# Four more pairs of projections by seven half products, and the order of their steps, in a one-core encoder layer

## The chip, the cores and the metric

The kernel runs on one core of one Trainium2 chip. The metric is the device time of one execution in microseconds (us). The engines of the core are named as in the profile: PE multiplies matrices (PEld is its weight load, which overlaps), DVE and ACT work element by element, POOL copies small things and issues the transfers that add to their destination, SP issues all other transfers.

## The reference: one encoder layer on 512 tokens

One post-norm layer of width 1024 on 512 tokens, in float32. Two attentions stand side by side, each has its own output projection, two sigmoid gates merge them, then come the output projection, a layer norm, a SwiGLU block of width 2816 and a second layer norm. Cut to what matters:

```python
proj = h @ w_in[l]                                   # 1024 -> 1536 (A) + 3 * 768 (B)
qa, ka, va, qb, kb, vb = jnp.split(proj, SPLITS, axis=-1)
qa, ka, qb, kb = rope_partial(...)                   # first 16 of each head's 64 columns
o_a = windowed_gqa_sink(qa, ka, va, a_sink[l])       # 16 heads, |i-j| <= 128, a sink per head
o_b = dilated_mixture(qb, kb, vb)                    # 4 slots x 3 dilations 1, 4, 16
g_a, g_b = jnp.split(jax.nn.sigmoid(h @ w_gate[l] + b_gate[l]), N_BRANCH, axis=-1)
mixed = g_a * (o_a @ w_br_a[l]) + g_b * (o_b @ w_br_b[l])
h = layer_norm(DN_ALPHA * h + mixed @ w_out[l], ln1_g[l], ln1_b[l])
f = (jax.nn.silu(h @ w_ff_gate[l]) * (h @ w_ff_up[l])) @ w_ff_down[l]
h = layer_norm(DN_ALPHA * h + f, ln2_g[l], ln2_b[l])
```

## The kernel before: a planned stream of matmuls

Every float32 operand of a product is split into a high part of reduced precision and the rest (a copy, mostly on ACT, then a subtraction on DVE), and a product of two of them is three matmuls: high by high, high by low, low by high. So each 128 by 512 piece of weights costs a transfer, a copy and a subtraction before PE can use it.

The weights lie packed in units of 128 output columns (a [128, 1024] block, two halves of 512). The projections of the first part of the layer come in two forms.

- A **plain unit** (`in_sbuf`, `dense_q`, `gate`, through `feat_x` and `feat_k`, L523 to L525) multiplies 8 pieces of 128 weights with all 512 tokens: 8 x 3 = 24 matmuls of 512 columns. Its weights are 4 tiles: two halves, each with a high and a low part.
- A **pair** (`pair_x`, L639 to L641) makes two units at once by Strassen's scheme on 2 x 2 blocks: seven products instead of eight, each of 4 x 3 = 12 matmuls of 256 columns, 84 in all. Before the products stand the sums of weight blocks: S1 and S3 are loaded as one block, to which a second transfer from POOL's queue adds another (`load_sum`, L387), S2 = S1 + A11 and S4 = A12 + S2 are DVE additions (`form`, through `tt`, L544), and seven operands are split (`parts`: ACT L373, DVE L544). Behind the products, four pieces are kept by ACT (`keep`, L647), and DVE joins them with one addition of 512 columns and one of 256 (L544, L662). The sums of token blocks are made once (`x_forms`).

Nothing in the program's order is written by hand line by line. Each operation is given to a list scheduler (`Program.op`) with its engine or engines, a cost, the tiles it reads and writes, and a due time: the PE time of all work noted so far (`pr.T`) plus an offset. Weights have an offset of -130 us, so they may be fetched and split that far ahead. `Program.run` then goes through a reckoned time and gives every free engine the ready operation with the earliest due time whose tiles find room; the resulting order of each engine is the program, and on the chip each engine keeps to it. Room is counted: 85 slots of [128, 512] float32, by classes (staging of weights `ws`, split weights `whl`, attention, the rest), and 8 PSUM banks by classes. Where a tile is counted in, `slab.tile` or `psum.tile` is called with one tag for all 85 slots or all 8 banks, and the pool chooses the place. The reckoned times include the transfers: on SP's queue `o.done = moved + (LATE if 95 < now < 150 else 2.4 ...)`, on POOL's 3.2 us (6.2 us late in the first part) behind the bytes.

The sequence of steps is the string `ORDER`: V, q and k of attention A (`VA`, `q1`, `k1`), its units `A0` to `A3`, pairs `P:`, turning of rows for the rotary part (`R`, `turn_rows`: 16 of each 64 rows of the tiles are gathered by SP, shuffled and multiplied by DVE, and put back by SP), the values of attention B (`V12`, `V0`), its units `B0` to `B3`, gates (`g`), fetching of A's output (`O`). Before the change it names eight pairs. Attention units issue small copies of the sink logits on POOL (L1020) ahead of their first scores, tied to the unit's first score matmul; scores, their reduction on DVE, the exponent on ACT, normalising, transposes on PE (L973, L988), splits and the product with the values follow one another.

Behind the first part come the branch projections (L523 to L525 with other operands), the output projection (L1480 to L1482), and the SwiGLU block, whose products by pairs of units (L1690 to L1692) and chunks (L1901 to L1903) are not touched.

## Time and profile before

| what | value |
|---|---|
| runs | 728.09, 728.14, 729.88 us; median 728.14 us |
| profiled execution, from its first to its last instruction | 725.8 us; the runs' median is 2.3 us longer |
| PE | 717.3 us busy, 99%, 4767 matmuls |
| DVE | 655.6 us busy, 90% |
| ACT | 471.4 us busy, 65% |
| POOL | 134.0 us busy, 18% |
| transfers | 140.30 MB, mean 193 GB/s |
| granted PE clock | 0.996 of full speed |

A matmul's busy time is from its start to a modelled end, and neighbours overlap, so what a matmul costs PE is the distance from its start to the next start, not its duration. DVE's and ACT's instructions overlap by some 0.1 us as well. "Idle" of an engine is a stretch minus its busy time in that stretch.

### The profile page before, as it was taken

To read this page: it belongs to the slowest core of one execution; us is meant where nothing else is said; L and a number is where in the kernel's file an instruction comes from. 1 tells how busy PE (TensorE), PEld (TensorE's weight loads), DVE (VectorE), ACT (ScalarE), POOL (GpSimd) and SP (SyncE) were. 2 spreads that over 40 slices of the span, in tenths; PEclk is the share of its full clock that TensorE was granted. 3 is DMA by queue.
4 is the path that set the end of the run, shared out by engine and by line. 5 is a ranking of instruction groups with operands and counts; after the bars stand their busy time and mean duration, and the time that the engine had idled before them with its cause. 6 is when DMAs were issued, how large, how long until landed. Compare 5 with 4: busy or idle time off the path is not lost.

```text
span 725.8 us, 14412 instructions
## 1 busy us (share of the span) xinstructions
PE 717.3 (99%) x4767; PEld 666.2 (92%) x4767; DVE 655.6 (90%) x1408; ACT 471.4 (65%) x1077; POOL 134.0 (18%) x297
## 2 busy tenths in 40 slices
PE   9999999999999999999999999999999999999995
PEld 7889999989988888988888999999999999999985
DVE  6999999889997898898967898899999999899987
ACT  5757798868778665666534666756666566666821
POOL 0021211111100731450020021111112211212000
PEclk9999999999999999999999999999999999999998
DMA  8978788856577689965681499676888888979302
GB/s 256 309 155 202 191 213 246 211 135 172 170 192 185 160 228 253 309 217 185 216 209 44 116 267 228 154 199 155 200 254 212 193 215 225 258 184 200 97 30 87
DMA packets 88010, 140.30 MB, mean 193 GB/s; under 512 B 11136, under 2 KB 24064, under 8 KB 87936
## 3 DMA queue, kind: packets, MB, share of 16 engines
q1 hardware_dynamic: 74336, 114.87, 51.7%
q0 software_dynamic: 13328, 24.39, 20.5%
q8 instruction: 37, 0.61, 0.3%
q14 instruction: 37, 0.30, 0.1%
q10 hardware_dynamic: 272, 0.13, 0.1%
HBM read 114.97 MB, written 7.60 MB: 169 GB/s over the span
## 4 chain that ended last, share of the span: by engine, by line
PE 99%; DVE 1%; DVEq 0%; issue 0%
PE ps L1692 10%; PE ps L1691 9%; PE ps L1690 9%; PE ps L523 9%; PE ps L524 9%; PE ps L525 9%; PE ps L1901 4%; PE ps L1903 4%; PE ps L1902 4%; PE ps L641 3%; PE ps L640 3%; PE ps L639 3%; PE ps L973 3%; PE ps L1480 3%; PE ps L1481 3%; PE ps L1482 3%
## 5 line engine op out<-in xcount | busy, mean ns | idle before, releaser
L373 ACT ACTIVATE sl<-sl 128x512 fp32r<-128x512 f32 (+3 forms) x419 | 230.8, 583 | 59.7 <-DVE sl L544 31.1
L544 DVE TENSOR_TENSOR sl<-sl,sl 128x512 fp32r<-128x512 f32 (+3 forms) x378 | 222.4, 621 | 5.1 <-ACT sl L373 3.4
L373 ACT ACTIVATE sl<-ps 128x256 f32<-128x256 f32 (+5 forms) x209 | 88.7, 445 | 91.6 <-PE ps L1692 56.8
L387 POOL DMA_DIRECT2D sl<-wpack x60 | 53.1, 885 | 342.9 <-DMA sl<-wpack 118.2
L1691 PE MATMUL ps<-sl,sl 128*128 128x256 f32 x352 | 96.8, 275 | 0.0
L1692 PE MATMUL ps<-sl,sl 128*128 128x256 f32 x352 | 96.8, 275 | 0.0
L1690 PE MATMUL ps<-sl,sl 128*128 128x256 f32 x352 | 96.8, 275 | 0.0
L523 PE MATMUL ps<-x,sl 128*128 128x512 f32 (+1 forms) x241 | 93.9, 389 | 0.0
L525 PE MATMUL ps<-x,sl 128*128 128x512 f32 (+1 forms) x241 | 91.4, 379 | 0.0
L524 PE MATMUL ps<-x,sl 128*128 128x512 f32 (+1 forms) x209 | 79.5, 380 | 0.0
L1690 PE MATMUL ps<-x,sl 128*128 128x256 f32 x264 | 72.6, 275 | 0.0
L1691 PE MATMUL ps<-x,sl 128*128 128x256 f32 x264 | 72.6, 275 | 0.0
L1692 PE MATMUL ps<-x,sl 128*128 128x256 f32 x264 | 72.6, 275 | 0.0
L1691 PEld LDWEIGHTS ps<-sl,sl 128*128 128x128 f32 x352 | 67.6, 192 | 0.1
L1690 PEld LDWEIGHTS ps<-sl,sl 128*128 128x128 f32 x352 | 67.6, 192 | 0.1
L1692 PEld LDWEIGHTS ps<-sl,sl 128*128 128x128 f32 x352 | 67.6, 192 | 0.0
L399 DVE TENSOR_TENSOR sl<-sl,sl 128x512 fp32r<-128x512 f32 x94 | 62.8, 682 | 1.8 <-ACT sl L373 1.3
L525 PEld LDWEIGHTS ps<-x,sl 128*128 128x128 f32 x241 | 45.9, 190 | 6.5
L1690 PEld LDWEIGHTS ps<-x,sl 128*128 128x128 f32 x264 | 50.6, 192 | 0.4
L1691 PEld LDWEIGHTS ps<-x,sl 128*128 128x128 f32 x264 | 50.6, 192 | 0.4
L523 PEld LDWEIGHTS ps<-x,sl 128*128 128x128 f32 x241 | 46.0, 191 | 5.4 <-ACT sl L373 0.3
L1692 PEld LDWEIGHTS ps<-x,sl 128*128 128x128 f32 x264 | 50.7, 192 | 0.0
(172 smaller groups left out, 1851.0 us busy)
## 6 DMA issues: line engine op xcount, KB each, us to landing
sl<-wpack SPq DMA_DIRECT2D x249, 256.0 KB, 3.9
sl<-wpack POOLq DMA_DIRECT2D x60, 256.0 KB, 5.3
sl<-sl SPq DMA_DIRECT2D x110, 128.0 KB, 3.1
wf<-wpack SPq DMA_DIRECT2D x51, 256.0 KB, 5.2
wf<-wpack POOLq DMA_DIRECT2D x24, 256.0 KB, 6.2
oa<-sl SPq DMA_DIRECT2D x32, 128.0 KB, 3.6
sl<-sl SPq DMA_DIRECT2D x68, 32.0 KB, 2.6
sl<-oa SPq DMA_DIRECT2D x8, 256.0 KB, 5.1
```

Source lines behind the costliest of these rows:

```text
L373: nc.scalar.activation(dst, src, AF.Copy)
L387: op([(POOL, 1.0)], lambda e: nc.gpsimd.dma_start(b.t, src2, accum_op=ALU.add), reads=[b], writes=[b], prio=prio, moves=1.65)
L399: op([(DVE, dve(S))], lambda e: nc.vector.tensor_tensor(l.t, src.t, f32(h.t), op=ALU.subtract), reads=[src, h], writes=[l], prio=prio, abs ...
L523: mm(o, a, x0, start=(k == 0 and begins), stop=False, skip_group_check=split)
L524: mm(o, a, x1, start=False, stop=False, skip_group_check=split)
L525: mm(o, b, x0, start=False, stop=(k == nk - 1), skip_group_check=split)
L544: op([(DVE, dve(w))], lambda e: nc.vector.tensor_tensor(dst(), x(), y(), op=o), reads=reads, writes=writes, prio=prio)
L1690: mm(o, wh, pairs(bh[k]()), start=(first and k == 0), stop=False, skip_group_check=True)
L1691: mm(o, wh, pairs(bl[k]()), start=False, stop=False, skip_group_check=True)
L1692: mm(o, wl, pairs(bh[k]()), start=False, stop=(k == 3), skip_group_check=True)
L1901: mm(ps.t, x0, pairs(w[0].t), start=(first and m == 0), stop=False, skip_group_check=True)
L1902: mm(ps.t, x0, pairs(w[1].t), start=False, stop=False, skip_group_check=True)
```

## The change

1. **Twelve pairs instead of eight.** The string `ORDER` is new. The eight units that were plain and are now in pairs are `q3`, `K10`, `Q10`, `Q11`, `Q12` and three gates; the twelve pairs are `q3,g`, `k1,q4`, `q5,Q01`, `q6,q7`, `g,g`, `g,Q00`, `g,K00`, `g,K01`, `Q02,K02`, `K10,Q10`, `Q12,Q11`, `g,g`. Two plain units of 24 matmuls of 512 columns each become one pair of 84 of 256, four times.
2. **Each step may carry an offset** (`@-471`) that is added to the due times of its operations while it is noted.
3. **Three pairs are marked `D:`.** Their sums S2 and S4 are not added by DVE but by a transfer from POOL's queue between two tiles in SBUF (`accum_op`, L624 of the new file), six in all. Two `r` steps gather the shuffled rows by 8-row transfers in place of DVE's shuffle.
4. **Transfers are reckoned longer**: the latency part by 1.3 while the reckoned time is under 380 us (`LONG`), and four transposes as 0.436 us instead of 0.36. These change the order that the scheduler makes, nothing else.
5. **Places are given out by the scheduler**: each of the 85 slots and 8 banks (and of the two small pools) has its own tag, and a tile is made in the place that has been free longest. Limits of some classes change by one or two.

New functions that no step of the new `ORDER` calls (`half_values`, a form of the last sums by transfers) are left out here.

```diff
-SPARE, SPARE2 = 12, 12
+SPARE, SPARE2 = (10, 12)
+LONG = 1.3
 ORDER = """
-VA q1 A0 q2 q3 g X P:k1,q4 R A1 P:q5,g P:q6,q7 R A2 P:g,g A3 P:g,g L P:Q00,K00 R V12 P:Q01,K01 R P:Q02,K02 R V0 B0 Q10 K10 R Q11 K11 R B1 O O Q12 K12 R O O B2 B3 O O O O g8
+q1@-471 X@-159 VA A0@-92 q2@-21 P:q3,g@-28 R@-36 D:k1,q4@-16 R@89 P:q5,Q01@-152 D:q6,q7@-32 r@680 D:g,g P:g,Q00@-10 L P:g,K00@-42 A1@-39
+R@180 V12@-5 P:g,K01@-30 R@22 P:Q02,K02@-15 R@-10 A2@-71 A3@-67 V0@36 P:K10,Q10@-17 B0@-44 O@-1217 O@-237 R@-587 K11@-20 B1@-33 P:Q12,Q11@-22
+R@-393 K12@-28 g@-17 O@-15 g@1 O@-37 g@13 P:g,g@-18 r@-237 O@-28 O@-26 B2@-290 O@62 g@12 g@-12 B3@-224 O@122 g@-26
 """
-FORMS = -60.0
-VAL = -100.0
-OA_AFTER = (0, 0, 0, 0, 0, 0, 0, 0)
+FORMS = -165.0
+VAL = -130.0
+OA_AFTER = (0, 0, 0, 0, 0, 1, 1, 0)
-N_WSA, N_WHLA = 8, 16
+N_WSA, N_WHLA = (8, 18)
...
                         if b.tile is None:
-                            b.tile = b.make()
+                            if b.keys[0] in self.rooms:
+                                b.room = self.rooms[b.keys[0]].popleft()
+                                b.tile = b.make(b.room)
+                            else:
+                                b.tile = b.make()
...
-                        o.done = moved + (LATE if 95 < now < 150 else 2.4 if 14 < now < SLOW else 0.87)
+                        o.done = moved + (LONG if now < 380 else 1.0) * (LATE if 95 < now < 150 else 2.4 if 14 < now < SLOW else 0.87)
...
-                        o.done = moved + (0.87 if e == ACT else 6.2 if ACC < now < 420 else 3.2 if 14 < now < SLOW else 2.2)
+                        o.done = moved + (LONG if now < 380 else 1.0) * (0.87 if e == ACT else 6.2 if ACC < now < 420 else 3.2 if 14 < now < SLOW else 2.2)
...
-        return Buf("slot", cls, lambda: slab.tile([P, S], dt, tag="slab", bufs=N_SLOT, name=name("sl")))
+        return Buf("slot", cls, lambda r: slab.tile([P, S], dt, tag=f"slab{r}", bufs=1, name=name("sl")))
...
         def form(key, of, x, y):
+            if by_dma:
+                a, b = W[of], W[x if y == of else y]
+                op([(POOL, 1.0)], lambda e: nc.gpsimd.dma_start(a.t, b.t, accum_op=ALU.add), reads=[a, b], writes=[a],
+                   prio=-LOOK, moves=1.65)
+                W[key] = a
+                return
             tt(lambda: W[of].t, lambda: W[x].t, lambda: W[y].t, ALU.add, [W[x], W[y]], [W[of]], S, -LOOK)
...
-        op([(PE, 0.36)], go, reads=[*toks, ident], writes=[pb])
+        op([(PE, 0.436)], go, reads=[*toks, ident], writes=[pb])
...
     for w in ORDER.split():
+        w, _, later = w.partition("@")
+        pr.T += float(later or 0)
         step(w)
+        pr.T -= float(later or 0)
```

How the rows move is shown at three places. In these rows a tile's number is its running number, `x` is a part of the tokens, `sl` a slot, `ps` a bank.

**PE, the first of attention B's later queries and keys.** Before, a plain unit (24 rows; those left out repeat these):

```order
L523 MATMUL ps_3171<-x_94,sl_2909 128x512
L524 MATMUL ps_3171<-x_103,sl_2909 128x512
L525 MATMUL ps_3171<-x_94,sl_2910 128x512
...
L523 MATMUL ps_3171<-x_242,sl_2947 128x512
L524 MATMUL ps_3171<-x_249,sl_2947 128x512
L525 MATMUL ps_3171<-x_242,sl_2948 128x512
```

Now the pair of a key and a query, in two banks:

```order
L659 MATMUL ps_3115<-x_98,sl_2787 128x256
L660 MATMUL ps_3115<-x_105,sl_2787 128x256
L661 MATMUL ps_3115<-x_98,sl_2788 128x256
...
L659 MATMUL ps_3147<-x_245,sl_2995 128x256
L660 MATMUL ps_3147<-x_253,sl_2995 128x256
L661 MATMUL ps_3147<-x_245,sl_2996 128x256
...
L659 MATMUL ps_3115<-sl_329,sl_3073 128x256
L660 MATMUL ps_3115<-sl_330,sl_3073 128x256
L661 MATMUL ps_3115<-sl_329,sl_3074 128x256
```

48 matmuls of 512 columns (two units) became 84 of 256, on seven split weight tiles in place of four. In the whole program PE has 192 rows of 128x512 less (1711 to 1519) and 336 of 128x256 more (2672 to 3008); transposes and all other rows are as many as before. The first 168 PE rows are the same, and the last 25 of PE, DVE, ACT and SP too.

**DVE, ahead of attention unit B0.** Before, two low parts of plain units between the rows of attention:

```order
L399 TENSOR_TENSOR sl_3413<-sl_3138,sl_3412 128x512
L978 TENSOR_TENSOR sl_3421<-ps_3405,sl_3420 128x512
...
L399 TENSOR_TENSOR sl_3482<-sl_3147,sl_3481 128x512
```

Now, at about the same place, low parts (L558 is L544 of before), and the two sums S2 and S4 of a pair (a slot that is read and written):

```order
L558 TENSOR_TENSOR sl_3780<-sl_3621,sl_3779 128x512
...
L558 TENSOR_TENSOR sl_3803<-sl_3693,sl_3802 128x512
...
L558 TENSOR_TENSOR sl_3621<-sl_3629,sl_3621 128x512
...
L558 TENSOR_TENSOR sl_3693<-sl_3693,sl_3621 128x512
L558 TENSOR_TENSOR sl_3851<-sl_3621,sl_3850 128x512
```

Ahead of B0's first product of dilated probabilities with values (L1162, now L1352), DVE had 558 rows and has 581: 22 more additions and subtractions of 512 columns, 4 more of 256, a few copies and shuffles less.

**POOL, attention unit A0 and the first two `D:` pairs.** Before, sink copies (L1020) and adding loads from memory:

```order
L1020 COPY sl_627<-nsink 128x1
L1020 COPY sl_630<-nsink 128x1
L387 DMA sl_663<-wpack 128x512
L387 DMA sl_747<-wpack 128x512
L387 DMA sl_881<-wpack 128x512
L387 DMA sl_953<-wpack 128x512
L1020 COPY sl_1086<-nsink 128x1
```

Now sums between tiles (L624) stand among the sink copies (L1208):

```order
L1208 COPY sl_856<-nsink 128x1
L1208 COPY sl_858<-nsink 128x1
L624 DMA sl_659<-sl_685 128x512
L401 DMA sl_830<-wpack 128x512
L624 DMA sl_727<-sl_756 128x512
L1208 COPY sl_975<-nsink 128x1
L1208 COPY sl_979<-nsink 128x1
L1208 COPY sl_981<-nsink 128x1
L624 DMA sl_688<-sl_659 128x512
L1208 COPY sl_996<-nsink 128x1
L624 DMA sl_773<-sl_727 128x512
```

`sl_659` becomes S2 of the first of these pairs, `sl_688` its S4, `sl_727` and `sl_773` those of the second. POOL issues 8 adding loads of weights more than before (60 to 68) and the 6 sums; SP has 545 rows against 521.

More of the change, by code (lines that the diff above doesn't have):

```diff
@@ L144, in __init__ @@
         self.strict = self.hold = False
+        self.rooms = {}
     @staticmethod
@@ L236, in run @@
                 _, _, b = heapq.heappop(frees)
+                if b.room is not None:
+                    self.rooms[b.keys[0]].append(b.room)
                 for key in b.keys:
@@ L342, in hybrid_layer @@
                   "ws": N_WSA, "whl": N_WHL0, "att": N_ATT, "gen": N_GEN,
-                  "unit": UNITS, "oa": N_OA, "st": 4, "x4": 4, "wf": N_WF})
+                  "unit": UNITS, "v": 4, "oa": N_OA, "st": 4, "x4": 4, "wf": N_WF})
+    pr.rooms = {k: deque(range(pr.limits[k])) for k in ("slot", "bank", "x4", "st")}
     op = pr.op
@@ L1333, in step @@
             op([(POOL, 0.0)], lambda e: pr.limits.update(ws=N_WS, whl=N_WHL), after=[env["mark"]])
-        elif w[:2] == "P:":
+        elif w[:2] in ("P:", "D:"):
             both = [units_of(x) for x in w[2:].split(",")]
-            for (u, f), t in zip(both, pair_x(*[u for u, _ in both])):
+            for (u, f), t in zip(both, pair_x(*[u for u, _ in both], w[0] == "D")):
                 if u < U_GATE:
```

227 lines of the change are left out of this document (202 added, 25 removed).

## The prediction

> **What bounds the kernel now.** I read the page's table of engines first, then the chain of waits and PE's own waits, then windows and pieces of the timeline.
>
> ```profile
> span 725.8 us, 14412 instructions
> ...
> PE 717.3 (99%) x4767; PEld 666.2 (92%) x4767; DVE 655.6 (90%) x1408; ACT 471.4 (65%) x1077; POOL 134.0 (18%) x297
> ...
> PE 99%; DVE 1%; DVEq 0%; issue 0%
> ```
>
> PE is 99% of the span and 99% of the chain that ended last. That alone does not show that it never waits; the list of PE's waits does, for it has one row, ahead of the first matmul (waiting line, what it waited for, us, times, longest):
>
> ```profile
> PE ps L459 <- DVE eps L510: 1.2, 1, 1.2
> ```
>
> So whatever other engines do, today they do it in PE's shadow, and a change is worth what it does to PE's rows, unless it brings PE its first wait. What a row costs PE is the distance between starts. Here are 19 steps of 256 columns in a pair, and five steps of 512 columns at the end:
>
> ```profile
> 100.86 0.28 PE L640 MATMUL ps<-sl,sl 128*128 128x256 f32 x1
> ...
> 102.98 0.28 PE L641 MATMUL ps<-x,sl 128*128 128x256 f32 x1
> ```
> ```profile
> 717.02 0.38 PE L1480 MATMUL ps<-sl,sl 128*128 128x512 f32 x1
> ...
> 718.10 0.38 PE L1482 MATMUL ps<-sl,sl 128*128 128x512 f32 x1
> ```
>
> 2.12 / 19 = 0.1116 us and 1.08 / 5 = 0.216 us. A row of 256 columns costs a little over half of one of 512 (2 x 0.1116 = 0.223), so seven half products in place of eight gain less than one eighth.
>
> **The pairs.** PE loses 192 rows of 512 and gains 336 of 256: 192 x 0.216 = 41.5 us off, 336 x 0.1116 = 37.5 us on, together **-4.0 us**. The last PE row of the program and all that follows it is untouched:
>
> ```profile
> 721.00 0.75 DVE sl L1543
> ```
>
> Without a new wait the span is 725.8 - 4.0 = 721.8 us. The runs' median lies 2.3 us above the profiled span, which I carry over: 724.1 us.
>
> **What DVE pays.** A pair has three more low parts than two plain units, two sums, and a joining addition of 512 and one of 256 columns. DVE's cost per row is again its step:
>
> ```profile
> 63.67 1.28 DVE L544 TENSOR_TENSOR sl<-sl,sl 128x512 f32<-128x512 f32 x2
> 64.88 0.48 DVE L1022 CUSTOM_DVE_ANT_0 sl<-ps,sl,nsink 128x256 f32<-128x256 f32 x1
> ...
> 67.81 0.42 DVE L662 SCALAR_TENSOR_TENSOR sl<-ps,sl 128x256 f32<-128x256 f32 x1
> 68.15 0.61 DVE L1022 CUSTOM_DVE_ANT_0 sl<-ps,sl,nsink 128x384 f32<-128x384 f32 x1
> ```
>
> 1.21 / 2 = 0.60 us for 512 columns, 0.34 for 256: (3 + 2 + 1) x 0.60 + 0.34 = 3.9 us a pair, 15.8 us for four. The six sums given to transfers take 3.6 of it back. Where this counts is the place to which most of it was moved: ahead of unit B0. Up to B0's first product of dilated probabilities, DVE's rows are 22 more of 512 and 4 more of 256 columns, and fewer copies and shuffles: 22 x 0.60 = 13.2, 4 x 0.34 = 1.4, less about 1.1, say +13.5 us. PE gets there at 264.1 us before (first row below); counting its rows ahead of that place at 0.1116 and 0.216, it gets there 4.0 us later now, at 268.1 (340 more of 256, 150 fewer of 512, 8 transposes and 8 short ones fewer). The windows show start, end, length, then the busy time of PE, PEld, DVE, ACT, POOL:
>
> ```profile
> 264.11 0.61 PE L1162 MATMUL ps<-sl,sl 128*128 128x256 f32 x4
> ```
> ```profile
> 0.00:20.00 20.00, 18.80 (x77) 14.65 (x78) 13.64 (x34) 12.65 (x28) 0.90 (x5) 1.00 0.84 268
> 20.00:60.00 40.00, 40.00 (x195) 35.11 (x194) 39.46 (x82) 23.98 (x47) 6.33 (x12) 1.00 0.80 220
> 60.00:140.00 80.00, 80.00 (x667) 78.60 (x666) 75.44 (x172) 69.02 (x167) 13.99 (x33) 1.00 0.81 212
> ```
> ```profile
> 20.00:264.00 244.00, 244.00 (x1617) 226.84 (x1616) 224.31 (x542) 187.62 (x459) 51.10 (x150) 1.00 0.74 195
> ```
> ```profile
> 420.00:680.00 260.00, 260.00 (x2037) 251.56 (x2037) 245.66 (x472) 167.82 (x361) 49.42 (x57) 1.00 0.82 207
> ```
>
> From 20 us to that place DVE was busy 224.3 of 244 us (91.9%), idle 19.7. Now it has 224.3 + 13.5 = 237.8 us of work and 248.1 us to do it in: it must be busy **95.9%** of the time, or PE waits there. In the long run DVE reaches 94.5% beside a PE that never waits (245.66 of 260), and 98.7% at its best (39.46 of 40), where split work lay ready far ahead. What ended its idle time in the stretch:
>
> ```profile
> DVE sl L978 <- ACT sl L373: 4.2, 6, 1.4
> DVE st L1029 <- ACT sl L1026: 2.5, 4, 0.8
> DVE sl L1022 <- PE ps L871: 2.2, 5, 0.7
> DVE sl L375 <- PE ps L973: 2.2, 4, 0.6
> DVE sl L715 <- DMA sl<-sl: 1.6, 2, 1.3
> ```
>
> Nearly all of it is attention's chain, where DVE was ahead and had no weights left to split within its room. The added rows are such weights, due up to 130 us ahead, so they can lie in those holes; I take it that most of the missing 4 points are found. If none are, the loss is the third rival below. I allow 0.7 us for what is not found: **724.8 us**.
>
> The new order leans on this more than the old one. The old plan reckoned four transposes at 0.36 us:
>
> ```profile
> 142.65 0.44 PE ps L973 x4
> ```
>
> With 192 transposes ahead of the place, 48 x 0.08 = 3.8 us by which PE came later on the chip than planned, a cover that the new plan, with 0.436, no longer has. The longer reckoned transfers give some cover back on loads, none on the chain of DVE and ACT.
>
> **ACT, SP, transfers, rooms: nothing.** ACT gets about 20 more copies of 512 columns and 16 of 256, and was idle 56 us of the 244. SP issues 24 more, and spent 90 us waiting for PE at one line alone (first row below). The pairs add 12 blocks of 262 KB and the sums 6, 4.7 MB on 62 MB by 300 us (208 GB/s); even with the transfer engines full, in the second row, PE kept its 36.00 of 36 us. New places for slots and banks cannot win on PE, which waits for no place; at worst a place is late in one queue, which I price with the small waits.
>
> ```profile
> SPq L381 <- PE ps L1692: 90.0, 69, 5.0
> ```
> ```profile
> 264.00:300.00 36.00, 36.00 (x199) 32.23 (x198) 30.54 (x83) 20.04 (x50) 5.80 (x10) 1.00 1.00 259
> 0.00:300.00 300.00, 298.81 (x1889) 273.72 (x1890) 268.49 (x657) 220.30 (x534) 57.80 (x165) 1.00 0.77 208
> ```
>
> **The sums by transfer.** The trace has none between two slots. The nearest rows are adding loads, from memory with weights and with A's output (median us to landing), and what stands around them on POOL (mean ns):
>
> ```profile
> sl<-wpack POOLq DMA_DIRECT2D x60, 256.0 KB, 5.3
> sl<-oa POOLq DMA_DIRECT2D x8, 256.0 KB, 7.5
> ```
> ```profile
> L387 POOL DMA_DIRECT2D sl<-wpack x60 | 53.1, 885 | 342.9 <-DMA sl<-wpack 118.2 <-DVE sl L544 54.1 <-DVE sl L399 39.6
> L1020 POOL COPY sl<-nsink 128x1 f32<-128x1 f32 x64 | 18.8, 361 | 80.0 <-PE ps L641 23.8 <-PE ps L1039 12.5 <-PE ps L973 11.8
> ```
>
> I take 7.5 us, the slower. PE's first 168 rows are unchanged, and the next starts here:
>
> ```profile
> 36.74 0.38 PE L523 MATMUL ps<-x,sl 128*128 128x512 f32 x1
> ```
>
> Counting on from there, A0's first score comes at 57.2. Four sink copies of 0.36 us behind it put the S2 sum (`sl_659`) at 59.0, its landing at 66.5, its split (ACT 0.6, DVE 0.7) at 67.8; PE wants it at 71.1. Cover 3.3 us. The S4 sum (`sl_688`) stands behind three copies of the next attention block, at 66.8, is ready at 75.6 and wanted at 80.4. Cover 4.8 us. With a landing L both are late once L is over 10.8: L - 10.8 for S2 and about L - 9.3 more for S4. Below 10.8 us the sums cost nothing, faster ones gain nothing; at twice the slower row, 15 us, they cost 9.9.
>
> The Trainium skill, page "DMA: Bandwidth & Descriptors", section "Anatomy of one DMA", fits 2.0 us plus bytes over 436 GB/s for a transfer of this queue; for 256 KB that is an estimate of 2.6 us, and by it the cover would be 5 us greater. The rows of this trace are two to three times that, so the measurement decides.
>
> **Rivals.**
>
> *DVE takes the gain back.* If DVE stays at the 94.4% of its dense stretches, its 237.8 us take 251.9, PE waits 3.8 us on the way to B0's product, and the time is 724.1 + 3.8 = 728.0: no change. For it: the missing cover above, and half of DVE's idle time is ACT's latency. Against it: 98.7% in 20 to 60 us.
>
> *DVE becomes the bound.* If the new rows fall on top of the old idle time (91.9%), 237.8 us take 258.8, PE waits 10.7 us, 734.8 us: slower. It decides below 93.5%. Against it: PE's products of pairs stand between attention's rows to be used as filling, and idle time for lack of work shrinks when work is added.
>
> *The sums land late*, at 15 us: 734.0 us, from 13 us on slower. Against it: no row of POOL's queue is near.
>
> *Weight loads become the bound.* PE gets 144 more loads, and 192 ns a load is longer than a step of 0.1116:
>
> ```profile
> L640 PEld LDWEIGHTS ps<-sl,sl x128: 189/192/192, 62.9 to 193.2; 128*128 128x128 f32 x128
> ```
> ```profile
> 420.00:440.00 20.00, 20.00 (x181) 20.00 (x181) 19.96 (x41) 14.87 (x31) 5.27 (x6) 1.00 0.98 257
> ```
>
> At one load after another, 336 x 0.192 - 41.5 = +23 us, 751 us. The window has 181 matmuls in 20 us with PEld full, so loads overlap each other too. The Trainium skill, page "TensorE: Matmul & The Clock Gate", section "Back-to-back issue gap", says that a stream of loads and matmuls runs at about 81 ns for 128 and 131 ns for 512 columns; on the line between, 256 columns give an estimate of 98 ns and the change would cost 336 x 0.098 - 192 x 0.131 = 7.8 us, 736 us, slower. The steps of 0.1116 and 0.216 in this trace disagree with it.
>
> **How the numbers follow.** Forecast (gain kept, waits under 1.8 us) 0.56; gain taken back 0.28; DVE the bound 0.09; late sums 0.05; weight loads 0.02. About 0.3%, 2.2 us, is what a measurement of this kernel can tell from no change, so faster is below 725.9 and slower above 730.3: 0.56, 0.28, 0.16. The likeliest case has 723.8 to 725.9 for its own; the range runs from 723.7, the sum without a wait and 0.4 for the spread of the runs, to 730.4, all of the second case, and leaves out 0.16 above.
>
> **What would show it.** PE's busy time 4.0 us less with its list of waits still empty, and DVE at or over 95% from 20 to 268 us: the forecast. PE rows waiting for DVE's L558 or L1166 around A and B units, with some 4 us in all: the second case; over 6 us, the third. Waits at L659 for ACT's splits behind L624: the sums. Steps of 256 columns over 0.112 us would undo the arithmetic itself.

## The result: 0.7% slower, and where the time went

| | before | after |
|---|---|---|
| median of the compared runs | 728.12 us | 732.86 us |
| profiled execution: its time, and its span | 728.09 us, 725.8 us | 732.64 us, 730.9 us |
| start of the last PE row | 718.10 us | 723.24 us |

The ratio is 1.0068, with a 95% interval of 1.0053 to 1.0083. The prediction said 724.8 us; the time lies above its range, and 8.1 us above the forecast.

The page of the changed kernel, its span, its engines and the shares of the chain that ended last:

```profile
span 730.9 us, 14814 instructions
...
PE 716.1 (98%) x4911; PEld 668.2 (91%) x4911; DVE 663.9 (91%) x1418; ACT 483.2 (66%) x1109; POOL 155.2 (21%) x311
...
PE 87%; DMA 5%; DVE 4%; SPq 2%; issue 1%; ACT 1%; DVEq 0%; ACTq 0%
```

PE's share of the chain fell from 99% to 87%, and transfers (DMA, 5%) and SP's queue of issues (SPq, 2%) stand there, which the list of before did not have. Most of those two, some 31 us, is the fetching of the first 33 us, to which the chain now leads back; the rest lies between 244 and 293 us. PE's list of waits (line, what it waited for, us, times, longest) had one row and has five:

```profile
PE ps L1352 <- DVE sl L1186: 2.9, 1, 2.9
PE ps L537 <- ACT sl L387: 1.7, 1, 1.7
PE ps L473 <- DVE eps L524: 1.2, 1, 1.2
PE ps L1161 <- DVE sl L1151: 1.2, 1, 1.2
PE ps L1161 <- ACT sl L1149: 0.2, 1, 0.2
```

The row of 1.2 us at L473 is the start of the program, as before. The list has waits only; what PE lost in all is found by taking its usual step from each distance between starts: 0.6 us at 40 to 46 us, 1.8 at 260 to 262 (the transposes, L1161), 2.1 at 284.8 to 287, 4.7 at 292.2 to 298.6, 0.5 at 402. So nearly all of it lies between 260 and 300 us. The windows show it (start, end, length, busy PE, PEld, DVE, ACT, POOL, PE clock, share of the transfer engines, GB/s). After:

```profile
20.00:240.00 220.00, 219.91 (x1602) 208.58 (x1601) 210.05 (x490) 177.70 (x427) 50.41 (x100) 1.00 0.87 220
237.00:283.00 46.00, 44.64 (x291) 40.78 (x290) 40.70 (x117) 32.56 (x95) 19.44 (x69) 1.00 0.78 188
283.00:300.00 17.00, 12.36 (x55) 10.14 (x54) 11.11 (x29) 11.18 (x26) 9.01 (x29) 0.90 1.00 314
```

Before:

```profile
20.00:240.00 220.00, 220.00 (x1487) 205.35 (x1486) 203.92 (x481) 169.74 (x410) 34.02 (x90) 1.00 0.74 196
237.00:283.00 46.00, 46.00 (x251) 41.20 (x250) 39.67 (x111) 31.38 (x79) 20.13 (x67) 1.00 0.79 203
283.00:300.00 17.00, 17.00 (x95) 15.20 (x94) 14.27 (x43) 7.74 (x22) 4.07 (x8) 1.00 1.04 286
```

Up to 240 us the new kernel does what it was forecast to do. From 283 to 300 us PE is busy only 12.4 of 17 us, and DVE (11.1) and ACT (11.2) are not full either; only the transfer engines are. SP's timeline of that stretch (start, us, line, how many issues) shows a queue with hardly a pause:

```profile
237.38 8.87 SPq L842 DMA_DIRECT2D sl<-sl  x12
246.31 3.23 SPq L732 DMA_DIRECT2D sl<-sl  x4
...
263.20 7.15 SPq L887 DMA_DIRECT2D sl<-sl  x8
270.46 6.46 SPq L842 DMA_DIRECT2D sl<-sl  x8
277.02 5.04 SPq L887 DMA_DIRECT2D sl<-sl  x8
...
282.74 1.86 SPq L395 DMA_DIRECT2D sl<-wpack  x4
284.77 0.33 SPq L1514 DMA_DIRECT2D sl<-oa  x1
285.20 0.86 SPq L395 DMA_DIRECT2D sl<-wpack  x2
```

L842 and L887 are **moves**: 64 rows of a query's or key's tile are moved from one slot to another, 128 KB each, so that a head's rows lie where the dilated scores want them. Behind 24 of them stand six loads of weights (L395) for plain units (L537 to L539): two for the unit that PE does from 286.8 us, four for units from 297 us on. 62 issues in the 45.4 us from 237.4 to 282.7 us are 0.73 us each. The scheduler reckoned 0.62, a difference of 7 us over all; five issues that stalled for 1.2 to 1.8 us make some 4.5 of them. (The kernel before had 64 issues in the same stretch, so their number is not what changed.) The scheduler's own reckoned times agree with PE's rows of this trace within 0.2 us up to 240 us, but the first of those six loads was reckoned to go out at 275.1 us and goes out at 282.7: SP is 0.7 us behind the plan at 237 us and 7.6 at 282.

The kernel before has a like queue in this stretch:

```profile
266.46 8.87 SPq L856 DMA_DIRECT2D sl<-sl  x8
275.38 1.86 SPq L723 DMA_DIRECT2D sl<-sl  x3
278.48 1.77 SPq L381 DMA_DIRECT2D sl<-wpack  x4
...
285.40 7.51 SPq L856 DMA_DIRECT2D sl<-sl  x8
...
294.09 5.91 SPq L381 DMA_DIRECT2D sl<-wpack  x9
```

But its four loads of 278.5 us serve products from 298.8 us on. The changed kernel's first load of 282.7 us serves the products at 286.8.

From there it is a chain in order of time. ACT's split of the first of these pieces, then PE (start, us; in brackets the idle time ahead and what ended it):

```profile
286.15 0.63 ACT L387 ACTIVATE sl<-sl 128x512 fp32r<-128x512 f32 x1 [3.69 <-DMA sl<-wpack]
...
292.62 0.63 ACT L387 ACTIVATE sl<-sl 128x512 fp32r<-128x512 f32 x1 [0.85 <-DMA sl<-wpack]
...
293.65 0.67 ACT L1444 ACTIVATE sl<-ps,bg 128x512 f32<-128x512 f32 x1
294.22 1.53 ACT L387 ACTIVATE sl<-ps 128x256 fp32r<-128x256 f32 x4
```
```profile
286.83 0.48 PE L537 MATMUL ps<-x,sl 128*128 128x512 f32 x1 [1.66 <-ACT sl L387]
...
292.20 0.38 PE L539 MATMUL ps<-x,sl 128*128 128x512 f32 x1
295.52 2.05 PE L1352 MATMUL ps<-sl,sl 128*128 128x256 f32 x8 [2.95 <-DVE sl L1186]
297.36 0.63 PE L537 MATMUL ps<-x,sl 128*128 128x512 f32 x1
297.79 0.63 PE L538 MATMUL ps<-x,sl 128*128 128x512 f32 x1
298.21 0.63 PE L539 MATMUL ps<-x,sl 128*128 128x512 f32 x1
```

The wait at 292.2 us names DVE, but DVE's operand (L1186) is the low part of what ACT copies at 294.22, and ACT keeps to its order: it stood at 292.62 for a piece of weights first. PE needs that piece only at 306.8 us; it holds up PE through ACT's order. In the chain of waits it is one row:

```profile
285.74 6.86 DMA sl<-wpack
```

Issued 285.74, landed 292.60. In freer stretches such a load lands about 3 us after its issue. The wait is followed by eight rows of 256 columns in 1.84 us (0.23 each in place of 0.1116) and rows of 512 columns at a distance of 0.42 instead of 0.216: half clock, 1.6 us more (the granted clock is 0.90 over 283 to 300 us). The wait at 260 us hangs on the same queue: the chain leads from it to ACT and back through the rotary part's transfers (landed at 253.6 and 260.6 us) to SP's issues from 244 us on.

### The profile page after: what moved, and what is told of

The parts are those of the page before. It is cut to its first block, busy times and chain, and to the rows that moved or that the text cites. A ratio compares the mean times of both kernels' runs of the same rounds, so it can differ in the third digit from the quotient of the medians.

```text
span 730.9 us, 14814 instructions
## 1 busy us (share of the span) xinstructions
PE 716.1 (98%) x4911; PEld 668.2 (91%) x4911; DVE 663.9 (91%) x1418; ACT 483.2 (66%) x1109; POOL 155.2 (21%) x311
## 4 chain that ended last, share of the span: by engine, by line
PE 87%; DMA 5%; DVE 4%; SPq 2%; issue 1%; ACT 1%; DVEq 0%; ACTq 0%
PE ps L1906 9%; PE ps L1905 9%; PE ps L1904 9%; PE ps L659 5%; PE ps L660 4%; PE ps L661 4%; PE ps L537 4%; PE ps L538 4%; PE ps L539 4%; PE ps L2115 4%; PE ps L2116 4%; PE ps L2117 4%; PE ps L1161 3%; PE ps L1694 3%; PE ps L1695 3%; PE ps L1696 3%
## 5 line engine op out<-in xcount | busy, mean ns | idle before, releaser
L387 ACT ACTIVATE sl<-sl 128x512 fp32r<-128x512 f32 (+3 forms) x437 | 242.0, 586 | 72.1 <-DVE sl L558 41.2
L558 DVE TENSOR_TENSOR sl<-sl,sl 128x512 fp32r<-128x512 f32 (+3 forms) x408 | 240.9, 627 | 2.7 <-ACT sl L387 1.7
L401 POOL DMA_DIRECT2D sl<-wpack x68 | 59.8, 880 | 373.0 <-DMA sl<-wpack 153.6
L387 ACT ACTIVATE sl<-ps 128x256 f32<-128x256 f32 (+5 forms) x206 | 85.5, 437 | 71.2 <-PE ps L1906 52.7
L1905 PE MATMUL ps<-sl,sl 128*128 128x256 f32 x352 | 96.8, 275 | 0.0
L1906 PE MATMUL ps<-sl,sl 128*128 128x256 f32 x352 | 96.8, 275 | 0.0
L1904 PE MATMUL ps<-sl,sl 128*128 128x256 f32 x352 | 96.8, 275 | 0.0
L537 PE MATMUL ps<-x,sl 128*128 128x512 f32 (+1 forms) x177 | 69.1, 390 | 1.7 <-ACT sl L387 1.7
L539 PE MATMUL ps<-x,sl 128*128 128x512 f32 (+1 forms) x177 | 67.4, 381 | 0.0
L413 DVE TENSOR_TENSOR sl<-sl,sl 128x512 fp32r<-128x512 f32 x78 | 52.8, 685 | 6.1 <-DMA sl<-wpack 3.4
L538 PE MATMUL ps<-x,sl 128*128 128x512 f32 (+1 forms) x145 | 55.2, 381 | 0.1
L558 DVE TENSOR_TENSOR sl<-sl,ps 128x512 f32<-128x512 f32 (+1 forms) x71 | 46.6, 661 | 8.2 <-PE ps L2117 5.3
L659 PE MATMUL ps<-sl,sl 128*128 128x256 f32 x192 | 53.6, 279 | 0.1
L661 PE MATMUL ps<-sl,sl 128*128 128x256 f32 x192 | 52.8, 275 | 0.0
L660 PE MATMUL ps<-sl,sl 128*128 128x256 f32 x192 | 52.8, 275 | 0.0
L1904 PEld LDWEIGHTS ps<-x,sl 128*128 128x128 f32 x264 | 50.6, 192 | 0.4
```

The source lines that it names most:

```text
L387: nc.scalar.activation(dst, src, AF.Copy)
L401: op([(POOL, 1.0)], lambda e: nc.gpsimd.dma_start(b.t, src2, accum_op=ALU.add), reads=[b], writes=[b], prio=prio, moves=1.65)
L537: mm(o, a, x0, start=(k == 0 and begins), stop=False, skip_group_check=split)
L538: mm(o, a, x1, start=False, stop=False, skip_group_check=split)
L539: mm(o, b, x0, start=False, stop=(k == nk - 1), skip_group_check=split)
L558: op([(DVE, dve(w))], lambda e: nc.vector.tensor_tensor(dst(), x(), y(), op=o), reads=reads, writes=writes, prio=prio)
```

## The experiments

Theory A: **the one queue of transfers** (SP's issues, and behind them the landings) bounds the stretch from 237 to 300 us, and the change left too little time there between a transfer's issue and its use (the expectations below call this theory S, T or A). Rivals: the places given to slots and banks; DVE's denser work.

### Taking a little from SP, and the places

`e1_pool16`: SP's 16 moves of L887 go out from POOL's queue. `e2_shuffle`: four of SP's gathers become one shuffle on DVE. `e3`: both. `e4`: the new order, but slots and banks come from shared tags again as before.

```diff
 e1 -                    op([(SP, 0.4)], lambda e, ...: nc.sync.dma_start(
 e1 +                    op([(SP, 0.4)], lambda e, ...: queue_of_move().dma_start(   # nc.gpsimd from the 17th move on
 e2 -                            nc.sync.dma_start(
 e2 +                            (nc.vector.stream_shuffle(h_(), g(), SHUF2) if last else None) if len(tiles) == 1 else nc.sync.dma_start(
 e4 -        return Buf("slot", cls, lambda r: slab.tile([P, S], dt, tag=f"slab{r}", bufs=1, name=name("sl")))
 e4 +        return Buf("slot", cls, lambda: slab.tile([P, S], dt, tag="slab", bufs=N_SLOT, name=name("sl")))
```

> The changed kernel, but the last 16 half moves of K (line 887, issued by SP at 263 to 282 us) are issued by POOL instead; the order on PE, DVE and ACT is word for word the same. Theory S (SP's queue is behind: it issued without a pause from 237 to 283 us, and the weight load that PE waits for at 284.8 us went out at 282.7): those 16 issues took 12.3 us of SP, so the loads go out near 271 us, PE's waits at 284.8 (2.1 us) and at 292.2 (4.7 us with the half clock behind it) vanish, 732.9 - 6.8 = 726.1 us; the wait at 260 us (1.8 us) stays. Theory D (DVE has too much work ahead of B0, as my rivals in the prediction had it): no change, 732 to 733.5. If POOL's issues land too late a new wait stands at B0's or B1's scores instead.

Measured 731.44 us, ratio 1.0045 (1.0030 to 1.0059): a miss. The loads went out at 275.4 us, not 271, since SP's own eight moves, with POOL's beside them, now took 11.15 us instead of 6.46:

```profile
263.56 11.15 SPq L842 DMA_DIRECT2D sl<-sl  x8
274.81 0.55 SPq L1521 DMA_DIRECT2D sl<-oa  x1
275.40 3.32 SPq L395 DMA_DIRECT2D sl<-wpack  x4
```

That is 1.4 us a move in place of 0.8. The wait at 285 us is gone, the one at 292 fell to 1.7, and new ones came at 269 (1.2 us) and at L1290 for a move itself (0.5). A second queue moved the loss more than it took it away. The Trainium skill says this of transfers in general (page "DMA: Bandwidth & Descriptors", sections "Issuing engines are not separate DMA queues" and "Rules for kernel authors"): other issuing engines save only issue time, since all transfers interleave on the same 16 engines. These rows agree, and here not even all of the issue time was saved.

> The changed kernel, but the last step r turns its rows with one shuffle on DVE, at the same place of the order, in place of four 8-row transfers of SP at 249.6 to 252.3 us. Theory S: SP is 2.7 us ahead from there on, so the transposes at 260 us no longer wait (-1.8), the load behind the wait at 284.8 comes 2.7 us sooner (-2.1) and the wait at 292.2 is shorter by some 2 to 3 us with its half clock: 726 to 728 us. Theory D: one more row of 0.6 us on an engine that is the bound, 733 to 734.

Measured 733.66 us, 1.0081 (1.0061 to 1.0100): a miss. SP was only 1 us earlier at 281 us, which did not reach its loads in time.

> Both of these edits at once. Theory S: all of PE's waits between 255 and 300 us go, 9.0 us less, 732.9 - 9.0 = 723.9 us, faster than the kernel before (728.1) by about the 4.0 us of the prediction's arithmetic. Theory D: 733 or more.

Measured 730.07 us, 1.0032 (1.0020 to 1.0044), a miss by 6 us; PE still lost 0.9 to 1.6 us each near 261, 276, 283 and 293 us.

> The changed kernel, but slots, banks and small tiles are given out by the pools from shared tags, as in the kernel before; the order on every engine is the same. Theory P (the places that the scheduler now gives out put waits into the queues): faster by up to the 9 us lost. Theories S and D: no change, 732 to 734 us.

Measured 734.14 us, 1.0094 (1.0077 to 1.0111), with the same wait of 3.1 us at L1351. So the places are not the cause.

### Putting moves behind the loads

Of the 24 moves at 263 to 282 us, 12 are first read by PE at 305 us or later, and 6 of the 12 at 237 to 246 us too. `e5` issues the 12 behind the loads, `e6` those 6 later as well. `put_off` keeps the issue back until SP's 378th issue; in `e6` also from the 300th to the 329th.

```diff
-        op([(SP, 0.4)], lambda e: nc.sync.dma_start(f32(dst.t[d:d + 64]), f32(src.t[c:c + 64])), reads=[src],
+        op([(SP, 0.4)], lambda e: put_off(c, lambda: nc.sync.dma_start(f32(dst.t[d:d + 64]), f32(src.t[c:c + 64]))), reads=[src],
```

> The changed kernel, but on SP's queue alone another order: 12 of the 24 half moves at 263 to 282 us, whose tiles PE first reads at 305 to 310 us, go out behind the seven loads at 282 to 286 us instead of ahead of them. Same transfers, same queue; PE, DVE, ACT and POOL have the same rows. Theory S (the loads are late because SP's queue is behind): the loads go out 8 us sooner, at 274.5 to 277.5, PE's waits at 284.8 (2.1 us) and at 292.2 (4.7 with the half clock) go, 732.9 - 6.8 = 726.1 us, faster than the kernel before. Theory B (the transfer engines are full from 284 us on, and it is the landing time there that holds PE, whatever the order): only the wait at 284.8 goes, 730.8. Theory D (DVE has too much work): no change.

Measured 730.77 us, 1.0037 (1.0025 to 1.0049). That is theory B's 730.8 by luck, for B had the wait at 292 us stay. The loads went out at 275 us and that wait vanished, but a new one stands at 284.9. The list of PE's waits, and DVE's row behind it:

```profile
PE ps L545 <- DVE sl L419: 3.8, 1, 3.8
```
```profile
288.12 0.69 DVE L419 TENSOR_TENSOR sl<-sl,sl 128x512 fp32r<-128x512 f32 x1 [5.31 <-DMA sl<-sl]
```

DVE's low part of the first weight piece was to lie in a slot that a put-off move still had to read. The cost went from the loads to the moves.

> As the run before, and also 6 of the 12 half moves at 237 to 246 us, which PE first reads at 305 us, go out behind the 8-row gathers of the last step r instead of ahead of them. Theory S: the gathers go out 4.9 us sooner, so the turned rows are back sooner and the transposes at 260.8 us no longer wait (1.8 us): 726.1 - 1.8 = 724.3 us. If the gathers wait for ACT's copies and not for SP, the wait at 260 us stays and the time is that of the run before. Theory D: no change, 733.

Measured 730.62 us, 1.0034 (1.0023 to 1.0045), a miss: the wait at 260 us fell to 0.5, those at 284 (2.4) and 292 (1) stay.

Three more variants try to avoid just that. `e9` issues the two moves that hold that slot first among those put off, `e10` puts off only six moves and not those, `e11` also two fetches of attention A's output (L1514).

> The run before last (e6) showed the loads out 9 us sooner and PE's wait at 292 us gone, but a new wait at 284.4 us: DVE's low part of a weight (line 419 there) is written to the slot from which a put-off move still had to read. So here only 8 moves of the K pairs are put off behind the loads, those first whose slot is wanted first, and the four of line 842 stay where they were; the 6 at 240 to 246 us are put off as in e6. Theory S with the place as the cause of the new wait: the loads go out 5.2 us sooner than in the changed kernel, at 277.5; no wait at 284 us, none or under 0.5 us at 292, under 0.5 at 260: 732.9 - 8.1 = 724.8 us, faster than the kernel before. If slots are not what held DVE in e6, the wait at 284 us stays at 2 us or more and the time stays near 730.5.

Measured 732.04 us, 1.0061 (1.0047 to 1.0075), a miss: the two moves landed at 288.3 and 288.7 us, 7.4 us after their issue, and the wait of 3.9 us stayed.

> The run before (e9) still had the wait near 285 us: the low part of the first load is written to the slot that two put-off moves still read, and these landed at 288.3 and 288.7 us, 7.4 us after their issue, behind the loads. Here those two stay ahead of the loads, and only 6 moves, whose slots are wanted from 286 us on, go out behind them; the group at 240 to 246 us stays as in the changed kernel. Theory S: the loads go out 3.9 us sooner, at 278.8 us; no wait at 284.8 (2.1 us), the last of the six loads lands near 288 in place of 292.6, so that of the wait at 292.2 and its half clock (4.7 us) under 1 us is left: 732.9 - 5.8 to 6.8 = 726 to 727 us. Theory B (the engines' transfers from 284 us on are the limit, whatever the order): the wait at 292 stays at 2 us or more, 730 or more.

Measured 730.97 us, 1.0044 (1.0029 to 1.0059). The wait at 285 us is gone; the last of the six loads landed 7.7 us after its issue and PE waited 2.4 us at 289 and 1.5 at 292. This is theory B's case: with the loads 4.6 us sooner in the queue it was their landing that PE waited for.

> As the run beside it, and two fetches of A's output (line 1514, at 282.1 and 284.8 us), whose data ACT first reads at 295.7 and 298.3 us, also go out behind the six loads and the six moves. Theory S and B together: 1.0 us sooner for all loads and two transfers of 256 KB fewer among them, so the last of the six lands near 286 to 287 us; both waits gone, 726 us; if the fetches now come late, a new wait of 1 to 3 us stands near 298 to 303 us.

Measured 736.44 us, 1.0121 (1.0104 to 1.0138). From 280 to 300 us PE lost 1 us only, and then 7.6 at once, because ACT stood for a fetch that had been put off. The wait came where it was expected, but at 7.6 us, not 1 to 3:

```profile
299.19 0.63 ACT L394 ACTIVATE sl<-sl 128x512 fp32r<-128x512 f32 x1 [7.63 <-DMA sl<-oa]
```

No order tried by hand got every transfer there in time.

### Giving SP more to do

If the queue is the bound of this stretch, more issues cost about their own time behind whatever reserve there is. `e7` adds 16 stores of 128 KB (10.4 us of SP) beside moves of the kernel before, `e8` 8 (5.2 us) to the changed one.

```diff
+        nc.sync.dma_start(dst, src)
+        n_moves[0] += 1
+        if 16 < n_moves[0] <= 32:          # 24 in e8
+            nc.sync.dma_start(dram.tile([64, S], F32, name=name("spare"))[:], src)
```

> The kernel before with 16 stores of half a slot to unused memory added on SP's queue, one behind each of the last 16 half moves of K (266 to 292 us): some 10.4 us more for SP and 2 MB. Nothing else is changed. Theory S: here SP has no pause either from 266 to 293 us, so the loads behind it at 294 us go out 10 us later than now; they were some 5 us ahead of need, and PE, which waits nowhere now, waits 4 to 6 us near 290 to 300: 728 + 5 = 733 us. Theory D: SP has room, no change, 728.

Measured 736.15 us, 1.0110 (1.0097 to 1.0123): 8.1 us more, not 5. So the kernel before, whose PE never waited, had a reserve of only 10.4 - 8.1, some 2 us, here. The first wait says the same: behind the first eight stores SP was 5.5 us later than before, and PE then waited 3.3. (The 8.1 us hold a half clock of some 1.7 us as well, and the last loads went out 11.0 us late.) The waits it gets are of the changed kernel's kind:

```profile
PE ps L1171 <- DVE sl L1007: 3.3, 1, 3.3
```

> The changed kernel with 8 such stores added on SP's queue, behind the moves at 263 to 270 us: 5.2 us more for SP ahead of the loads that PE waits for. Theory S: the waits at 284.8 and 292.2 us grow by most of that, 732.9 + 4 to 5 = 737 to 738 us. Theory D: no change, 733.

Measured 738.65 us, 1.0139 (1.0125 to 1.0152): 5.8 us more for 5.2 us of issues. The changed kernel, which already waits here, has no reserve. But some 3.4 of the 5.8 us are half clock (the granted clock is 0.5 for 10.2 us in all, against 3.4), and the largest of the new waits (L1292, 3.1 us) is for moves, not for the loads.

### Taking 18 moves away

`e12` is the changed kernel without 18 of the moves between SP's 305th and 378th issue, `e13` the kernel before without 18 of its own in the same stretch. These 18 moves are not issued and the products read other rows in their place, so the scores of those blocks are other numbers; PE, DVE, ACT and POOL keep every row.

```diff
+        if group == 0 and LEFT_OUT[0] <= pr.n_sp < LEFT_OUT[1]:
+            left_out.add(t)
+            return
         go()
```

> The changed kernel without 18 of the 36 half moves that SP issues from 237 to 282 us; it leaves out the first half of the heads' parts there, and their products read the second half's tiles, so the scores of those blocks are other numbers, while every row of PE, DVE, ACT and POOL is the same. No slot is held longer than before. Theory T (what sets the end from 237 to 300 us is the one queue of transfers; every order of it tried so far made another transfer late): 18 x 0.65 us of issuing and 2.4 MB less leave it 12 us to spare, all of PE's waits from 255 to 300 us go (9.0 us), 732.9 - 9.0 = 723.9 us, which is what the prediction's arithmetic gives for PE alone. If PE still waits 3 us or more there, something else than the transfers holds it.

Measured 724.79 us, 0.9948 (0.9932 to 0.9964): **8.1 us faster than the changed kernel, for 18 transfers** (7.8 when each is set against the kernel before in its own runs). The span, PE's waits and the windows:

```profile
span 721.7 us, 14787 instructions
...
PE 712.2 (99%) x4911; PEld 666.4 (92%) x4911; DVE 663.0 (92%) x1418; ACT 483.1 (67%) x1109; POOL 158.6 (22%) x311
```
```profile
PE ps L476 <- DVE eps L527: 1.2, 1, 1.2
PE ps L540 <- ACT x L390: 0.8, 1, 0.8
```
```profile
20.00:268.00 248.00, 248.00 (x1794) 235.12 (x1793) 236.03 (x559) 198.68 (x487) 68.78 (x158) 1.00 0.85 216
283.00:300.00 17.00, 17.00 (x94) 15.28 (x93) 16.36 (x50) 13.63 (x32) 14.04 (x34) 1.00 0.91 289
```

Both waits that are left lie in the first 6 us. The loads went out at 270.1 us. DVE is busy 236.0 of 248 us there, 95.2%, and PE does not wait for it, so DVE is not the bound.

> The kernel before without the like 18 of its last 36 half moves (243 to 292 us), leaving out the same part. PE waits nowhere in the kernel before, so by every theory no change: 728.1 us within 0.5. It shows that e12's gain, if there is one, is the change's lost gain and not a general one.

Measured 727.79 us, 0.9995 (0.9986 to 1.0004): no change. The same relief is worth nothing where the queue has its 2 us of reserve. How much of the 8.1 us belongs to the issues, how much to the 2.4 MB less on the transfer engines and how much to products that need not wait for a move, these two do not tell apart. The moves left out are the first halves, some of which PE reads within 5 us of their issue in the changed kernel.

### As many moves by another engine

These take the other 18 of the 36 moves, the second halves, which PE reads first at 305 to 310 us. `e14` makes them as copies on POOL, `e15` on ACT, `e16` 12 on POOL and 6 on ACT; everything is computed, in the order the changed kernel has.

```diff
+        if group == 64 and COPIED[0] <= pr.n_sp < COPIED[1]:
+            if BY[len(pr.n_copied) % len(BY)] == "POOL":
+                nc.gpsimd.tensor_copy(dst, f32(src))
+            else:
+                copy(ACT, dst, f32(src))
```

> The changed kernel, with 18 of the 36 half moves of 237 to 282 us (those that PE first reads at 305 to 310 us) done by a copy on POOL in place of a transfer; all else, and what is computed, as in the changed kernel. POOL is idle 26.6 of the 46 us there. Theory T: the transfers are as few as in e12, so 724.8 us if POOL's copies of 64x512 take 1 us or less each and hold up none of its small copies that DVE waits for; each us by which they do costs about as much, so up to 730.

Measured 729.29 us, 1.0023 (1.0014 to 1.0033), the best of the versions that compute all, and 3.6 us below the change's median (3.0 when each is set against the kernel before in its own runs). A copy takes POOL 0.75 us, and POOL keeps to its order too, in front of small copies (L1320) for which DVE waits. POOL's group from 237 to 300 us, and DVE's wait:

```profile
L847 POOL CAST sl<-sl 64x512 fp32r<-64x512 f32 x18 | 13.5, 749 | 1.6 <-issue 0.6
```
```profile
DVE st L1327 <- POOL st L1320: 3.1, 2, 2.0
```

> The same 18 moves as copies on ACT, 0.53 us each, 9.5 us in all at 237 to 282 us, where ACT was busy 32.6 of 46 us. Theory T: 724.8 us plus what ACT's later rows lose: attention's exponentials wait behind the copies, and their margin at PE is under 1 us, so 725 to 728 us, faster than the kernel before all the same.

Measured 732.32 us, 1.0061 (1.0046 to 1.0075), a miss: a wait of 2.7 us came at 269, ACT being in the chain of attention.

> The same 18 moves, the first 6 (240 to 246 us) on ACT, which was busy only 4.2 of 10 us at 250 to 260, the other 12 (263 to 282 us) on POOL. Theory T: 724.8 us plus under 1 us of new waits near 250 us, 725 to 726 us, if POOL's copies are as in e14.

Measured 730.84 us, 1.0041 (1.0028 to 1.0054), a miss: the largest loss is 2.4 us at 278, at L1174 for ACT, with a half clock behind it.

### A plan that knows the queue

All of these keep the order that the changed kernel's scheduler made while it reckoned 0.62 us an issue. `e17` lets it reckon 0.80 us a move and 0.62 a load from 232 to 285 us, with the steps' offsets sought anew against such a queue; `LONG` goes back to 1.0, and SP still makes every move. `e18` does likewise (0.78 us a move, from 226 to 320 us, `LONG` still 1.3) and may give any move to POOL.

```diff
 e17 -                        end = now + (0.62 if 14 < now < SLOW else 0.47)
 e17 +                        hot = T0 < now < T1
 e17 +                        end = now + ((MV if cost <= 0.4 else LD) if hot else 0.62 if 14 < now < SLOW else 0.47)
 e18 +        op([(SP, 0.4), *BESIDE], lambda e: half(e, dst.t[d:d + 64], src.t[c:c + 64]), reads=[src],
```

> The scheduler reckons the queue of transfers about as it ran: 0.80 us for an issue of a move between slots and 0.62 for a load (they took 0.73 on average from 237 to 282 us, with stalls), between 232 and 285 us; the steps' offsets were then sought again so that PE waits least under such a queue. Every move is still made, by SP. Theory A (the one queue is the bound; the change failed since its plan reckoned the queue too fast, and a plan that knows could put the work around it): the last PE row starts at 716 to 720 us instead of 723.2, time 726 to 730, ratio 0.997 to 1.003. Theory B (zero sum: there is simply not enough of the queue from 237 to 300 us, whatever order is made): waits of 3 to 5 us come back at some other line between 260 and 310 us, 730 to 733 us, as all reorderings by hand did.

Measured 730.46 us, 1.0034 (1.0020 to 1.0047). The time lies just above theory A's range and inside B's, but B's waits are not there: PE waits nowhere from 237 to 300 us, though every transfer of the change is made.

```profile
237.00:283.00 46.00, 46.00 (x331) 43.32 (x330) 43.16 (x114) 36.17 (x100) 26.49 (x73) 1.00 0.94 251
283.00:300.00 17.00, 17.00 (x89) 15.18 (x88) 12.73 (x26) 11.07 (x21) 2.03 (x4) 1.00 0.95 214
```

So there is enough of the queue for the work in this stretch, when its issues are spread as SP's timeline shows: four loads go out at 262.5 us, and 16 of the moves only from 288.7 us on.

```profile
262.46 1.81 SPq L397 DMA_DIRECT2D sl<-wpack  x4
...
288.67 6.21 SPq L889 DMA_DIRECT2D sl<-sl  x8
295.00 5.45 SPq L844 DMA_DIRECT2D sl<-sl  x8
```

But the gain isn't kept. In its profiled execution (728.53 us, the lowest of its runs) the last PE row starts at 719.0 us, 5.0 later than in `e12`: counted row by row against PE's usual steps, about 2.2 us are lost in small gaps from 30 to 100 us, 0.9 between 210 and 340, 1.7 ahead of and in the layer norm (396 to 406), 0.4 at 463. In the list of waits the norm's is the largest one:

```profile
PE ps L1777 <- DVE sl L1759: 1.4, 2, 0.8
```

The offsets were moved for one stretch, and the new order costs others. Its runs spread to 733.8 us, more than those of before; what the slower ones lose is not seen, since the profiled one is the fastest.

> As the other one, and each of the halves' moves may be made by POOL as a copy of 64x512 (0.75 us measured) wherever the scheduler finds POOL free, so that the queue has fewer of them and no fixed set is tied to POOL's place in its order. Theory A (the one queue is the bound and a relief of it that costs no other chain keeps the pairs' gain): last PE row at 715 to 718 us, time 725 to 728, ratio 0.995 to 1.000. Theory B (POOL's copies stop DVE or its own chain again, as where 18 moves were given to it by place): waits of DVE for POOL of 2 us and more, time 729 to 731.

Measured 733.57 us, 1.0074 (1.0061 to 1.0087): a miss for both theories. PE lost 2.5 us at 257 to 261 (transposes, the first at L1170 for ACT), 0.8 each at 279 and 295, and 1.7 at the norm; DVE's waits for POOL are 1.5 us in this stretch, less than the rival said.

None of the versions that compute everything beats the kernel before.

## Why the prediction was wrong, step by step

- **"PE never waits, so a change is worth what it does to PE's rows, unless it brings PE its first wait."** Right as a rule; it brought the wait.
- **The pairs, -4.0 us, span 721.8 us without a new wait.** Right: `e12`, where the queue is relieved, has a span of 721.7 us and its last row at 714.0 (718.1 - 4.0 = 714.1). The steps are still 0.1116 and 0.216 us. That its time (724.79) equals the forecast to the digit is luck: the 0.7 us allowed for DVE did not come, and this execution lies 3.1 us above its span, not 2.3.
- **DVE at 95.9% up to 268 us, most of the missing points found, 0.7 us for the rest.** Right: 95.2% in `e12` without a wait. Both rivals on DVE fall. (PE gets to B0's product at 267.2 us there, not 268.1: the trace has 328 more rows of 256 columns ahead of it, not 340.) I had taken DVE for the nearest limit since it was the busiest engine beside PE; where a wait names it, it had itself been held up by a transfer.
- **The sums by transfer, cover of 3.3 and 4.8 us at a landing of 7.5.** Right: their median landing is 6.3 us, and no row at L659 waited for their splits.
- **"ACT, SP, transfers, rooms: nothing."** This is the step that failed, and in it the sentences on SP and on the transfers. The 90 us that SP spent waiting belong to a line (L1692) of the SwiGLU block behind 400 us; in the stretch that the change touches, SP of before issues almost without a pause from 224 us to 300 (9 us of pauses, the longest 2.5). Nor were its additional issues 24; the traces have 34 (586 to 620). And that PE kept 36.00 of 36 us with the transfer engines full showed that there was enough, not that anything was over. `e7` measured what was over: about 2 us. The part of the step on places was right (`e4`), and so was that on ACT's load; ACT's fixed order, though, handed the late loads on to PE.
- **The cover that the old plan had by reckoning its transposes short.** I named it, 3.8 us, and charged its loss to DVE's chain alone, saying that the longer reckoned transfers would give some back on loads. The new plan raised the latency of a transfer, while what was short was the reckoned *issue*: 0.62 against 0.73 us. Set beside the traces, the plans say this: before, SP was 7 to 11 us behind its plan at 282 to 294 us and PE 4.9, which hid about half; now SP is 7.6 us behind at 282.7 and PE 2. And the new plan left less to begin with: it sends the first of the six loads out 7.9 us ahead of PE's row, where the old one had 25 us or more for the loads of this stretch and 11 for the tightest of its moves. So the queue's lag is not new; the cover over it is gone. This is worked out from the plans' times, and how much each part matters was not measured; the 2 us of reserve is.

So the term that was missing is the queue's, 732.86 - 724.79 = 8.1 us by `e12`, priced at 0. None of the four rivals held the case that came.

## What to carry to other kernels

Read an engine's or a queue's idle time in the very stretch that the change touches: a total over the program can come from another stage altogether. A queue that issues without a pause while PE is full has a reserve that no busy share shows; a few extra issues in front of what PE needs measure it in one run. Beside the number of transfers, compare how long before its use each one goes out. And where one error of a planner may be hidden by another, look for the second before mending the first.

## What the runs showed of the hardware

- **An issue of a small move costs more than that of a large load.** A move of 128 KB between slots takes SP 0.59 us and 0.05 us between two, a gather of 8 rows 0.63, a load of 256 KB 0.33 to 0.54 (nine in ten). Five issues between 237 and 283 us stalled for 1.2 to 1.8 us, three of them while adding transfers from POOL's queue ran and two not; what stalls them stays open.
- **Eight transfers of SP are under way at most,** for the program gives them eight semaphores in turn: from 288 us on, each next issue of the changed kernel starts within 0.1 us of the landing of the one eight before it. With the engines full that turns landings of 6.9 to 8.5 us (2.3 for a move and about 3 for a load when free) into later issues.
- **A wait of PE can cost more than itself.** Gaps of 3.1 us (the changed kernel), 3.9 (`e9`), 4.0 (`e5`), and also of 2.8 (`e15`) and 2.4 (`e16`), were followed by rows at half rate, 0.42 us in place of 0.216, with a granted clock of 0.5 for 3.4 us; after one of 4.7 in `e2` it was 6.8 us. A gap of 2.4 us in `e6` and one of 1.9 in `e1` were not followed by any. So length alone does not decide. The Trainium skill, page "TensorE: Matmul & The Clock Gate", Part 1, has the half clock after an idle window of about 3.4 us that runs free of the kernel's own time. That the same gap can end either way agrees with a free-running window; that 2.4 us were enough once does not agree with its length, and the measurement decides.
